# Attention probabilities and the residual transposed by VectorE blocks and strided DMA instead of TensorE

## The chip, the cores and the metric

The kernel runs on one core of one Trainium2 chip. The metric is the device time of one execution in microseconds (us). TensorE (PE in the profile) does the matrix products, VectorE (DVE) and ScalarE (ACT) the elementwise work, and SyncE (SP) issues nearly all DMAs; GpSimd (POOL) has next to nothing to do here. Each engine works through its own list of instructions in the order in which they were written down when the kernel was built, and an instruction that waits holds up all that stand behind it in that list.

## What is computed

Two layers of a sequence model on a sequence of 512 tokens of width 1024, each with an RMS norm ahead and a residual addition behind: first a state space mixer, then a latent attention mixer with 16 heads, and one more RMS norm at the end. The change is in the second layer. Cut to what matters:

```python
def mla_mixer(u, positions, in_w, q_norm_w, kv_norm_w, uq_w, ukv_w, out_w):
    proj = u @ in_w
    c_q, c_kv, k_r, z = proj[..., :o1], proj[..., o1:o2], proj[..., o2:o3], proj[..., o3:]
    q = (rms_norm(c_q, q_norm_w) @ uq_w).reshape(bsz, seq, 16, 192)
    kv = (rms_norm(c_kv, kv_norm_w) @ ukv_w).reshape(bsz, seq, 16, 256)
    ...
    o = causal_block_attention(q_full, k_full, v, 192 ** -0.5)   # p = softmax(q k^T); o = p v
    o = o.reshape(bsz, seq, 2048) * jax.nn.silu(z)
    return o @ out_w

h = h + mla_mixer(rms_norm(h, w), ...)
return rms_norm(h, final_norm_w)
```

## The kernel before, in words

All data are float32. A matrix product is made of three passes over parts `hi` and `lo` of its operands: ACT casts `hi`, DVE subtracts it from the source to get `lo`. This holds for weights (`split_weight`, tiles `raw`, `whi`, `wlo`) and for activations.

The first layer and the input projections work with features on the 128 partitions and the 512 tokens along the free dimension. The residual `h` (eight tiles of 128 features x 512 tokens) must be turned to tokens on partitions before the output projection, because `out_tok` makes its output that way. Before the change this is done in `mla`, in the loop over the six tiles of the first projection: behind each of the last four, eight transposes on PE through the identity matrix (line 682) go into two PSUM banks `pt`, ACT copies them to `ht` (L685), and SP writes `ht` to the DRAM buffer `hd` (L686). `out_tok` reads it back as `hr` (L924).

Attention works head by head. `score(h, b)` computes the scores of query block b (128 queries, b = 0 to 3) against keys 0 to 128(b+1), takes the softmax on DVE and ACT, and leaves the normalised probabilities `p` with queries on partitions. `product(h, kb)` needs them with keys on partitions. `turn(h, kb)` does this for key block kb: 4 - kb transposes on PE (L818, so 10 for a head) into a PSUM bank `pt`, then ACT casts `ph` (L822) and DVE subtracts to get `pl` (L823). Three matmuls of `product` (L836) then use `ph`, `pl` and the values `va`, `vb`.

The order of PE's instructions is written out by hand: PE's list is the order of the program text. The main loop runs over heads h = 0 to 15. An iteration feeds large matmuls (`front_a` or `front_b`, the projections for the next pair of heads, and `zgemm`, the gate; from head 11 on also the output projection), and `sched` puts pieces between them at fixed shares of the iteration: the scores of head h+1 at the shares `SC`, the turns of head h at `TU`, the products of head h at `PR`. `SF` holds the places of the scores of head 0. An iteration with even h has `front_a`, which also contains a rotation of half the query (`rope`): a PSUM result is copied to `rraw` (L732), four DMAs swap its quarters into `rsw` (L697), and DVE combines the two. An iteration with odd h has `front_b`.

The lists of DVE, ACT and SP are put in order by a scheduler at build time. On SP stand the weight loads (L263: `raw` has two buffers, and is free again once `wlo` is made), the DMAs of `rope` and those of `hd`.

Of the kernel before, what the change touches and what calls it, by code (L numbers as in the profile page):

```python
# [10 lines left out]
F32 = mybir.dt.float32  # L11
F32R = mybir.dt.float32r
AF = mybir.ActivationFunctionType
ALU = mybir.AluOpType

P = 128
T = 512
D = 1024
KD = D // P
NCH = T // P  # L20
# [3 lines left out]
MH = 16  # L24
QL, KVL = 384, 256
# [14 lines left out]
P1 = (1.0, 2.4, 3.8, 12.0, 18.2)  # L40
GN = 16.84
G7 = 33.0
SF = (0.02, 0.1, 2.1, 3.1)
SC = (0.0, 0.16, 0.25, 0.44)
TU = (0.02, 0.08, 0.38, 0.55)
PR = (0.3, 0.48, 0.65, 0.94)
KO = (3, 4, 5, 8, 10)
MID = 4
NU = 1
# [102 lines left out]
class Net:  # L152
# [497 lines left out]
    def mla(self):  # L650
        tc, nc, t, wk = self.tc, self.nc, self.t, self.wk
        v = nc.vector
# [3 lines left out]
        nc.sync.dma_start(con[:], t["con"][:, K_MASK:])  # L656
        self.mask, self.cosT, self.sinT = con[:, 0:T], con[:, T:2 * T], con[:, 2 * T:3 * T]
        hd = self.dram.tile([NCH, P, D], F32, name="hd")
        vh, vl = [], []
        for k in range(KD):  # L660
            h = self.h[k]
            a = self.act.tile([P, T], F32R, tag="ah", name=self.nm("vh"))
            b = self.act.tile([P, T], F32R, tag="al", name=self.nm("vl"))
# [6 lines left out]
        for i in range(6):  # L670
            w = self.weight("w", U_M1 + i)
            ps = self.bank("mm")
            self.run(self.gemm(ps[:], w, vh, vl, KD))
            if i == NU:
                pss = self.sumsq([h[:] for h in self.h], D, "b")
                r1 = self.rstd_of(pss, D)
            if i >= 2:
                c = i - 2
                for n in range(2):
                    pt = self.bank("pt")  # L680
                    for k in range(4):
                        nc.tensor.transpose(pt[:, k * P:(k + 1) * P], self.h[4 * n + k][:, c * P:(c + 1) * P],
                                            self.ident)
                    ht = wk.tile([P, T], F32, tag=("ph", "pl")[n], name=self.nm("ht"))
                    nc.scalar.copy(ht[:], pt[:])  # L685
                    nc.sync.dma_start(hd[c, :, n * T:(n + 1) * T], ht[:])  # L686
            pend.append(ps)
            while pend and i >= NU:
                o = self.o16.tile([P, T], F32, tag="o", name=self.nm("cq"))
                v.tensor_tensor(o[:], pend.pop(0)[:], r1[:], op=ALU.mult)  # L690
                cq.append(o)
# [15 lines left out]
        def zgemm(i):  # L707
            w = self.weight("w", U_MZ + i)
            ps = self.bank("mm")
            yield from self.gemm(ps[:], w, vh, vl, KD)  # L710
            z = self.o16.tile([P, T], F32, tag="o", name=self.nm("z"))
            v.tensor_tensor(z[:], ps[:], r1[:], op=ALU.mult)
            zt.append(z)
            yield 8 * 0.216
# [36 lines left out]
        def front_b(j):  # L751
            f = F[j]
            w = self.weight("ub", j)
            ps = self.bank("mm")
            yield from self.gemm(ps[:], w, qh, ql, 3)
            f["q", 1] = self.split(ps[:], "q", wk)
            yield 0.2
            ps = self.bank("mm")
            yield from self.gemm(ps[:], w, kh, kl, 2, 384)
            f["k", 1] = ksplit(ps[:])  # L760
            yield 1.3
            wh, wl = self.weight("uc", j)
            f["v"] = []
            for half in range(2):
                ps = self.bank("mm")
                for c2 in range(2):
                    c = 2 * half + c2
                    s = slice(c * P, (c + 1) * P)
                    seq = []
                    for k in range(2):  # L770
                        wc = slice(k * 256, k * 256 + 256)
                        seq += [(kh[k][:, s], wh[:, wc]), (kh[k][:, s], wl[:, wc]), (kl[k][:, s], wh[:, wc])]
                    for i, (a, b) in enumerate(seq):
                        nc.tensor.matmul(ps[:, c2 * 256:(c2 + 1) * 256], a, b, start=i == 0, stop=i == 5)  # L774
                va = wk.tile([P, T], F32R, tag="va", name=self.nm("va"), bufs=3)
                vb = wk.tile([P, T], F32R, tag="vb", name=self.nm("vb"), bufs=3)
                nc.scalar.copy(va[:], ps[:])
                v.tensor_tensor(vb[:], ps[:], va[:].bitcast(F32), op=ALU.subtract)
                f["v"].append((va, vb))
                yield 1.3  # L780

        probs = [[] for _ in range(MH)]

        def score(h, b):
            f, i = F[h // 2], h % 2
            (qa, qb), kk = f["q", i], f["k", i]
            r = f["r", i]
            n = P * (b + 1)
            s = slice(b * P, (b + 1) * P)
            ps = self.bank("s")  # L790
            if b:
                seq = [(qa, kk[:, 0]), (qa, kk[:, 1]), (qb, kk[:, 0]), (r, k1), (r, k2)]
                for k, (x, y) in enumerate(seq):
                    nc.tensor.matmul(ps[:, :n], x[:, s], y[:, :n], start=k == 0, stop=k == 4)  # L794
            else:
                both = ps[:, :2 * P].rearrange("p (a t) -> p a t", a=2)
                nc.tensor.matmul(both, qa[:, s], kk[:, :, :P], start=True, stop=False)
                nc.tensor.matmul(ps[:, :P], qb[:, s], kk[:, 0, :P], start=False, stop=False)
                nc.tensor.matmul(both, r[:, s], k12[:, :, :P], start=False, stop=True)
            p = self.res.tile([P, n], F32, tag="res", name=self.nm("p"))  # L800
            st = wk.tile([P, 4], F32, tag="st", name=self.nm("st"), bufs=8)
            mask = self.mask[:, T - n:]
            if b == 0:
                v.tensor_tensor(p[:], ps[:, P:2 * P], mask, op=ALU.add)
                mask = p[:]
            v.tensor_tensor_reduce(p[:], ps[:, :n], mask, -SCALE, 3.0e38, ALU.add, ALU.min, st[:, 0:1])  # L806
            self.E(p[:], p[:], AF.Exp, scale=-1.0, bias=st[:, 0:1], accum_out=st[:, 1:2])
            v.reciprocal(st[:, 2:3], st[:, 1:2])
            v.tensor_scalar(p[:], p[:], st[:, 2:3], None, op0=ALU.mult)
            probs[h].append(p)  # L810

        parts, acc = [[] for _ in range(MH)], {}

        def turn(h, kb):
            n = T - kb * P
            pt = self.bank("pt")
            for b in range(kb, NCH):
                nc.tensor.transpose(pt[:, (b - kb) * P:(b - kb + 1) * P], probs[h][b][:, kb * P:(kb + 1) * P],  # L818
                                    self.ident)
            ph = wk.tile([P, T], F32R, tag="ph", name=self.nm("ph"))  # L820
            pl = wk.tile([P, T], F32R, tag="pl", name=self.nm("pl"))
            nc.scalar.copy(ph[:, :n], pt[:, :n])  # L822
            v.tensor_tensor(pl[:, :n], pt[:, :n], ph[:, :n].bitcast(F32), op=ALU.subtract)  # L823
            parts[h].append((ph, pl))

        def product(h, kb):
# [13 lines left out]
        def chain(*gs):  # L840
            for g in gs:
                yield from g
# [4 lines left out]
            yield from self.out_tok(zt, 0, hd)  # L847

        def norm(tiles, n, cw):
            at = (wk, ("qh", "ql", "s2") if n == KVL else ("ph", "pl", "s2"))  # L850
            pss = self.sumsq([x[:] for x in tiles], n, "b", *at)
            r = self.rstd_of(pss, n, *at)
            hs, ls = [], []
            for i, x in enumerate(tiles):
                v.scalar_tensor_tensor(x[:], x[:], col(cw + i), r[:], op0=ALU.mult, op1=ALU.mult)
                a = wk.tile([P, T], F32R, tag="ch", name=self.nm("ch"), bufs=5)
                b = wk.tile([P, T], F32R, tag="cl", name=self.nm("cl"), bufs=5)
                nc.scalar.copy(a[:], x[:])
                v.tensor_tensor(b[:], x[:], a[:].bitcast(F32), op=ALU.subtract)
                hs.append(a)  # L860
                ls.append(b)
            return hs, ls
# [3 lines left out]
        qh, ql = norm(cq[:3], QL, C_QW)  # L866
# [14 lines left out]
        self.run(zgemm(3))  # L881
        zsilu(0)
        self.run(fa)
        self.run(front_b(0))
        self.sched(zgemm(4), [(x, functools.partial(score, 0, b)) for b, x in enumerate(SF)])
        for h in range(MH):
            if h and h % 4 == 0:
                zsilu(h // 4)
            feed, cost = [], 0.0
            j = h // 2 + 1  # L890
# [6 lines left out]
            if h >= 11:  # L897
                k = KO[h - 11]
                feed.append(itertools.islice(outg, k))
                cost += 1.3 * k  # L900
            at = SC if h + 1 < MH else ()
            pieces = [(x * cost, functools.partial(score, h + 1, b)) for b, x in enumerate(at)]
# [169 lines left out]
```

## Time and profile before

| | before |
|---|---|
| median of 3 runs | 840.51 us (840.49 to 840.99) |
| the profiled execution's own time | 840.15 us |
| its span in the profile | 838.3 us |
| PE, DVE, ACT busy, share of the span | 98%, 76%, 54% |
| DMA queue of SP (q1), share of 16 engines' span | 32.9% |
| granted TensorE clock | 0.998 |

The span is the time from the first to the last instruction in the profile; the execution's own time is 1.85 us longer. A busy share says how long an engine worked, not that the end depends on it. The chain of waits follows the end back from event to event and says which engine the time hangs on. A row of a list by line gives the line, the engine, the operation, the tile that is written and those that are read, shapes and count, then busy time and mean duration of one; a row of the timeline gives start, length and what ran; SPq is the issuing of DMAs on SP. The attention loop stands between about 500 and 784 us.

### The profile page before, as it was taken

The page shows a single profiled execution, that of the slowest core. Times are in us where ns is not written, and L with a number is a line of the kernel's source. Part 1 is how long each engine was busy: PE and PEld are TensorE (multiplying, and loading weights), DVE is VectorE, ACT ScalarE, POOL GpSimd, SP SyncE. Part 2 cuts the span into 40 slices and gives each one's busy share as a digit, 9 for nine tenths or more (in the row PEclk, how much of TensorE's full clock was granted, in tenths as well). Part 3 has the DMA queues.
Part 4 walks back from the last instruction along what each step waited for, and adds up shares of the span by engine and source line. Part 5 has one row for each costly group of instructions (what it writes and reads, how often), then busy time and mean ns, then how long its engine had stood idle before and what let it go on. Part 6 is the DMA issues. An engine that isn't in the chain of part 4 may idle for free.

```text
span 838.3 us, 11586 instructions
## 1 busy us (share of the span) xinstructions
PE 822.8 (98%) x4260; PEld 694.8 (83%) x4260; DVE 640.2 (76%) x1226; ACT 453.5 (54%) x802; POOL 0.2 (0%) x4
## 2 busy tenths in 40 slices
PE   7999999999999999999999999999999999999996
PEld 5887888888888888888888888888888888888885
DVE  7899898979788979776564887786767869675544
ACT  7567755545565657333354664456547557554233
POOL 0000000000000000000000000000000000000000
PEclk9999999999999999999999999999999999999999
DMA  6354543434242424323225242222221224331212
GB/s 227 102 186 145 153 150 106 147 101 128 98 151 76 151 87 137 121 95 101 90 86 176 79 129 64 77 65 73 73 64 56 89 75 157 100 100 53 92 59 100
DMA packets 35112, 90.55 MB, mean 108 GB/s; under 512 B 4784, under 2 KB 6320, under 8 KB 35056
## 3 DMA queue, kind: packets, MB, share of 16 engines
q1 hardware_dynamic: 34336, 88.77, 32.9%
q10 hardware_dynamic: 720, 1.05, 0.3%
q8 instruction: 33, 0.54, 0.3%
q14 instruction: 23, 0.19, 0.1%
HBM read 83.12 MB, written 4.33 MB: 104 GB/s over the span
## 4 chain that ended last, share of the span: by engine, by line
PE 91%; DVE 5%; DMA 2%; ACT 1%; issue 1%; SPq 0%; DVEq 0%; ACTq 0%
PE mm L291 54%; PE ot L942 11%; PE s L794 5%; PE mm L300 4%; PE po L836 4%; PE mm L774 3%; PE pt L818 2%; PE yd L138 2%; PE yd L291 1%; PE aux L130 1%; PE aux L105 1%; DMA x<-in_x_dram 1%; PE aux L77 1%; PE aux L89 1%; DMA L<-ac_d 1%; DVE wlo L273 1%
## 5 line engine op out<-in xcount | busy, mean ns | idle before, releaser
L272 ACT CAST whi<-raw 128x1024 fp32r<-128x1024 f32 (+3 forms) x132 | 127.0, 965 | 214.7 <-PE mm L291 177.4
L273 DVE TENSOR_TENSOR wlo<-raw,whi 128x1024 fp32r<-128x1024 f32 (+3 forms) x132 | 146.8, 1115 | 56.1 <-ACT whi L272 55.8
L291 PE MATMUL mm<-ah,whi 128*128 128x512 f32 x384 | 153.9, 401 | 0.0
L291 PE MATMUL mm<-ah,wlo 128*128 128x512 f32 x384 | 150.1, 391 | 0.4 <-DVE wlo L273 0.4
L291 PE MATMUL mm<-al,whi 128*128 128x512 f32 x384 | 149.8, 390 | 0.0
L291 PE MATMUL mm<-vh,whi 128*128 128x512 f32 x224 | 89.6, 400 | 0.9 <-ACT whi L272 0.9
L291 PE MATMUL mm<-vh,wlo 128*128 128x512 f32 x224 | 87.8, 392 | 0.7 <-DVE wlo L273 0.7
L291 PE MATMUL mm<-vl,whi 128*128 128x512 f32 x224 | 87.5, 391 | 0.0
L291 PEld LDWEIGHTS mm<-ah,wlo 128*128 128x128 f32 x384 | 72.1, 188 | 16.0 <-DVE wlo L273 0.8
L291 PEld LDWEIGHTS mm<-ah,whi 128*128 128x128 f32 x384 | 72.2, 188 | 15.5 <-issue 1.4
L291 PEld LDWEIGHTS mm<-al,whi 128*128 128x128 f32 x384 | 72.2, 188 | 14.4 <-DVE al L312 0.3
L942 PE MATMUL ot<-whi,ah 128*128 128x512 f32 (+1 forms) x136 | 52.3, 384 | 0.0
L942 PE MATMUL ot<-whi,al 128*128 128x512 f32 (+1 forms) x136 | 51.4, 378 | 0.0
L942 PE MATMUL ot<-wlo,ah 128*128 128x512 f32 (+1 forms) x136 | 51.4, 378 | 0.0
L291 PEld LDWEIGHTS mm<-vh,wlo 128*128 128x128 f32 x224 | 42.0, 188 | 10.8 <-DVE wlo L273 1.5
L291 PEld LDWEIGHTS mm<-vh,whi 128*128 128x128 f32 x224 | 42.1, 188 | 9.2 <-ACT whi L272 1.1
L223 ACT ACTIVATE p<-p,st 128x128 f32<-128x128 f32 (+1 forms) x64 | 36.1, 564 | 25.1 <-DVE st L806 25.0
L291 PEld LDWEIGHTS mm<-vl,whi 128*128 128x128 f32 x224 | 42.2, 188 | 7.2
L822 ACT CAST ph<-pt 128x512 fp32r<-128x512 f32 (+1 forms) x64 | 26.5, 422 | 33.2 <-PE pt L818 32.8
L291 PE MATMUL mm<-ch,whi 128*128 128x512 f32 x104 | 42.6, 409 | 0.0
L291 PE MATMUL mm<-ch,wlo 128*128 128x512 f32 x104 | 40.8, 392 | 0.0
L291 PE MATMUL mm<-cl,whi 128*128 128x512 f32 x104 | 40.7, 392 | 0.0
(225 smaller groups left out, 1642.6 us busy)
## 6 DMA issues: line engine op xcount, KB each, us to landing
raw<-in_w_dram SPq DMA_DIRECT2D x100, 512.0 KB, 3.3
L<-ac_d SPq DMA_DIRECT2D x32, 256.0 KB, 3.8
E<-ea_d SPq DMA_DIRECT2D x32, 128.0 KB, 3.3
raw<-in_ua_dram SPq DMA_DIRECT2D x8, 512.0 KB, 3.3
raw<-in_ub_dram SPq DMA_DIRECT2D x8, 320.0 KB, 2.9
x<-in_x_dram SPq DMA_DIRECT2D x8, 256.0 KB, 4.3
res<-in_x_dram SPq DMA_DIRECT2D x8, 256.0 KB, 3.3
hd<-ht SPq DMA_DIRECT2D x8, 256.0 KB, 2.3
```

The costliest lines, as they stand in the source:

```text
L138: nc.tensor.matmul(yd[64 * h:64 * h + 64, s], self.xdt[j][:, c, h, :], self.L[2 * j + h][:, s], start=True, stop=True)
L223: i = self.nc.scalar.activation(out, in_, func, **k)
L272: nc.scalar.copy(hi[:, a:b], raw[:, a:b])
L273: nc.vector.tensor_tensor(lo[:, a:b], raw[:, a:b], hi[:, a:b].bitcast(F32), op=ALU.subtract)
L291: self.nc.tensor.matmul(ps, a, b, start=i == 0, stop=i == len(seq) - 1)
L300: self.nc.tensor.matmul(p, seq[i][0], seq[i][1], start=i == 0, stop=i == 3 * ks - 1)
L774: nc.tensor.matmul(ps[:, c2 * 256:(c2 + 1) * 256], a, b, start=i == 0, stop=i == 5)
L794: nc.tensor.matmul(ps[:, :n], x[:, s], y[:, :n], start=k == 0, stop=k == 4)
L818: nc.tensor.transpose(pt[:, (b - kb) * P:(b - kb + 1) * P], probs[h][b][:, kb * P:(kb + 1) * P], self.ident)
L822: nc.scalar.copy(ph[:, :n], pt[:, :n])
L836: nc.tensor.matmul(po[:, kb * P:], x, y, start=kb == 0 and k == 0, stop=kb == NCH - 1 and k == 2)
L942: nc.tensor.matmul(ps[:, a:b], x, y, start=start and i == 0, stop=stop and i == 5)
```

## The change

The transposes on PE go. A block of probabilities `p` is turned in blocks of 32 x 32 by one DVE instruction into a new tile `pb` (two buffers); this leaves each 32 x 32 block turned in its place, and four DMAs for each `pb`, one for each 32 partitions, write the blocks to their places in a DRAM buffer `pd` (one for even, one for odd heads) as pieces of 32 floats, 128 bytes each. `turn` reads a key block of `pd` into `pl` with one DMA; ACT casts `ph` from it, and DVE makes `pl` in place. `pl` now has one buffer for each kb. The residual goes the same way: eight DVE transposes of 128 x 512 and 32 DMAs of 128-byte pieces into `hd`, spread over the same loop. The tables move: the scores of the next head stand earlier in an iteration, the products later. The scores of head 0 move from `zgemm(4)` into `front_b(0)`. The temporary tiles of the query's norm use other tags.

```diff
-SF = (0.02, 0.1, 2.1, 3.1)
-SC = (0.0, 0.16, 0.25, 0.44)
-TU = (0.02, 0.08, 0.38, 0.55)
-PR = (0.3, 0.48, 0.65, 0.94)
+SF = (0.6, 1.0, 2.0, 3.2)
+SC = (0.0, 0.1, 0.18, 0.28)
+TU = (0.04, 0.14, 0.4, 0.6)
+PR = (0.52, 0.66, 0.8, 0.96)
...
+        turned = hd[:].rearrange("c (j a) d -> a (c j) d", a=32)
...
             if i >= 2:
-                c = i - 2
-                for n in range(2):
-                    pt = self.bank("pt")
-                    for k in range(4):
-                        nc.tensor.transpose(pt[:, k * P:(k + 1) * P], self.h[4 * n + k][:, c * P:(c + 1) * P],
-                                            self.ident)
-                    ht = wk.tile([P, T], F32, tag=("ph", "pl")[n], name=self.nm("ht"))
-                    nc.scalar.copy(ht[:], pt[:])
-                    nc.sync.dma_start(hd[c, :, n * T:(n + 1) * T], ht[:])
+                for k in (2 * i - 4, 2 * i - 3):
+                    ht = wk.tile([P, T], F32, tag="ph", name=self.nm("ht"))
+                    v.transpose(ht[:], self.h[k][:])
+                    for b in range(4):
+                        m = slice(32 * b, 32 * b + 32)
+                        nc.sync.dma_start(turned[:, :, k * P + 32 * b:k * P + 32 * b + 32],
+                                          ht[m, :].rearrange("a (j b) -> a j b", b=32))
...
-        probs = [[] for _ in range(MH)]
+        pd = [self.dram.tile([T, T], F32, name=f"pd{i}") for i in range(2)]
...
-            probs[h].append(p)
+            pb = wk.tile([P, T], F32, tag="pb", name=self.nm("pb"))
+            v.transpose(pb[:, :n], p[:])
+            turned = pd[h % 2][:].rearrange("(j a) q -> a j q", a=32)
+            for i in range(4):
+                q = b * P + 32 * i
+                nc.sync.dma_start(turned[:, :n // 32, q:q + 32],
+                                  pb[32 * i:32 * i + 32, :n].rearrange("a (j q) -> a j q", q=32))
...
         def turn(h, kb):
             n = T - kb * P
-            pt = self.bank("pt")
-            for b in range(kb, NCH):
-                nc.tensor.transpose(pt[:, (b - kb) * P:(b - kb + 1) * P], probs[h][b][:, kb * P:(kb + 1) * P],
-                                    self.ident)
+            pl = wk.tile([P, n], F32R, tag=f"pl{kb}", name=self.nm("pl"), bufs=1)
+            nc.sync.dma_start(pl[:].bitcast(F32), pd[h % 2][kb * P:(kb + 1) * P, kb * P:])
             ph = wk.tile([P, T], F32R, tag="ph", name=self.nm("ph"))
-            pl = wk.tile([P, T], F32R, tag="pl", name=self.nm("pl"))
-            nc.scalar.copy(ph[:, :n], pt[:, :n])
-            v.tensor_tensor(pl[:, :n], pt[:, :n], ph[:, :n].bitcast(F32), op=ALU.subtract)
+            nc.scalar.copy(ph[:, :n], pl[:].bitcast(F32))
+            v.tensor_tensor(pl[:], pl[:].bitcast(F32), ph[:, :n].bitcast(F32), op=ALU.subtract)
...
-            at = (wk, ("qh", "ql", "s2") if n == KVL else ("ph", "pl", "s2"))
+            at = (wk, ("qh", "ql", "s2"))
...
-        self.run(front_b(0))
-        self.sched(zgemm(4), [(x, functools.partial(score, 0, b)) for b, x in enumerate(SF)])
+        self.sched(chain(front_b(0), zgemm(4)), [(x, functools.partial(score, 0, b)) for b, x in enumerate(SF)])
```

SP's list in the iteration of head 6, an even one, had only weight loads and the four DMAs of `rope` before:

```order
L263 DMA raw_5729<-in_ub_dram 128x640
L263 DMA raw_5848<-in_uc_dram 128x512
L263 DMA raw_5909<-in_w_dram 128x1024
L697 DMA rsw_5775<-rraw_5773 32x512 x4
L263 DMA raw_5991<-in_ua_dram 128x1024
```

In the same iteration SP now has the following list, in which `pd_4157` is the buffer of head 7, written in four sets of four, and `pd_4156` that of head 6, read as `pl`:

```order
L263 DMA raw_5823<-in_ub_dram 128x640
L814 DMA pd_4157<-pb_5847 32x4x32 x4
L822 DMA pl_5853<-pd_4156 128x512
L814 DMA pd_4157<-pb_5870 32x8x32 x4
L696 DMA rsw_5881<-rraw_5879 32x512 x4
L822 DMA pl_5895<-pd_4156 128x384
L814 DMA pd_4157<-pb_5919 32x12x32 x4
L814 DMA pd_4157<-pb_5944 32x16x32 x4
L822 DMA pl_5960<-pd_4156 128x256
L263 DMA raw_5965<-in_uc_dram 128x512
L822 DMA pl_5988<-pd_4156 128x128
L263 DMA raw_6017<-in_w_dram 128x1024
```

The reads of head 6 stand between the writes of head 7: the third read is behind 16 writes and the four DMAs of `rope`. This is so in the iterations of heads 0, 2, 4, 6, 8 and 10, and without `rope` in that of head 13; in that of head 11 the last read alone is behind the writes. In the other odd iterations all four reads of a head stand ahead of the 16 writes of the next one.

On PE, where the scores of the first query block stand in the same iteration, seven transposes for key blocks 0 and 1 followed before:

```order
L797 MATMUL s_5742<-k_5590,qh_5579 128x256
L798 MATMUL s_5742<-k_5590,ql_5580 128x128
L799 MATMUL s_5742<-k_4353,s_1075_5410 128x256
L818 MATMUL pt_5753<-ident,p_5552 128x128
L818 MATMUL pt_5753<-ident,p_5599 128x128
L818 MATMUL pt_5753<-ident,p_5611 128x128
L818 MATMUL pt_5753<-ident,p_5674 128x128
L818 MATMUL pt_5762<-ident,p_5599 128x128
L818 MATMUL pt_5762<-ident,p_5611 128x128
L818 MATMUL pt_5762<-ident,p_5674 128x128
```

The scores of the second block follow at once now:

```order
L796 MATMUL s_5836<-k_5682,qh_5671 128x256
L797 MATMUL s_5836<-k_5682,ql_5672 128x128
L798 MATMUL s_5836<-k_4339,s_1072_5488 128x256
L793 MATMUL s_5858<-k_5682,qh_5671 128x256 x2
L793 MATMUL s_5858<-k_5682,ql_5672 128x256
L793 MATMUL s_5858<-k_4339,s_1072_5488 128x256 x2
```

Nothing else is taken out of PE's list in an iteration. At its end, the products of key blocks 2 and 3 (`pl_5960` and `pl_5988` are what SP reads above) now stand next to each other:

```order
L291 MATMUL mm_5971<-vh_3866,wlo_5826 128x512
L838 MATMUL po_5978<-ph_5962,va_5762 128x256
L838 MATMUL po_5978<-ph_5962,vb_5763 128x256
L838 MATMUL po_5978<-pl_5960,va_5762 128x256
L838 MATMUL po_5978<-ph_5990,va_5762 128x128
L838 MATMUL po_5978<-ph_5990,vb_5763 128x128
L838 MATMUL po_5978<-pl_5988,va_5762 128x128
```

In this even iteration the products of blocks 2 and 3 are the last of PE's work, behind all of `zgemm`.

## The prediction

> **What bounds the kernel now.** I read the page's busy times first, then its chain of waits by engine, then PE's waits.
>
> ```profile
> PE 822.8 (98%) x4260; PEld 694.8 (83%) x4260; DVE 640.2 (76%) x1226; ACT 453.5 (54%) x802; POOL 0.2 (0%) x4
> PE 91%; DVE 5%; DMA 2%; ACT 1%; issue 1%; SPq 0%; DVEq 0%; ACTq 0%
> PE mm L300 <- ACT whi L272: 4.8, 1, 4.8
> PE mm L291 <- DVE wlo L273: 1.0, 3, 0.5
> ```
>
> PE is busy for 98% of the span, 91% of the chain lies on it, and its two longest waits (total, times, longest) come to 5.8 us, one of them with 4.8 us at the start. In the attention loop it does not wait at all. So what is taken out of PE's list shortens the time, as long as nothing new makes PE wait; and every new wait costs in full.
>
> **What the change removes.** The transposes' price is read from the chain, where each piece is the time that PE's list moves on, not from the mean duration, since matmuls overlap.
>
> ```profile
> 443.03 0.87 PE pt L682 x8
> 507.71 0.12 PE s L797
> 508.06 0.76 PE pt L818 x7
> 515.14 0.22 PE pt L818 x2
> 519.80 0.11 PE pt L818
> 524.72 0.12 PE s L797
> ```
>
> Eight transposes of the residual take 0.87 us, and the ten of a head 0.76 + 0.22 + 0.11 = 1.09 us: 0.109 us each. There are 32 + 160 = 192 of them, so PE loses 192 x 0.109 = **20.9 us** of work. The two rows of L797 mark the same place in two iterations: an even one lasts 17.0 us, and without its transposes 15.9 us. If all that is new were hidden, 840.15 - 20.9 = 819 us would remain.
>
> **What it adds on DVE and ACT.** A transpose in DVE does not occur in the trace. The nearest rows read and write the same shapes in SBUF, one input:
>
> ```profile
> L809 DVE TENSOR_SCALAR p<-p,st 128x512 f32<-128x512 f32 x16 | 7.7, 481 | 0.2
> L809 DVE TENSOR_SCALAR p<-p,st 128x128 f32<-128x128 f32 x16 | 4.4, 278 | 0.0
> L823 DVE TENSOR_TENSOR pl<-pt,ph 128x512 fp32r<-128x512 f32 x16 | 11.0, 690 | 3.7 <-ACT ph L822 3.7
> L312 DVE TENSOR_TENSOR al<-z,ah 128x512 fp32r<-128x512 f32 x16 | 10.8, 686 | 9.4 <-ACT ah L311 9.4
> 549.00:567.00 18.00, 18.00 (x103) 15.74 (x103) 15.53 (x36) 9.80 (x21) 0.00 (x0) 1.00 0.23 73
> 567.00:584.00 17.00, 17.00 (x93) 14.71 (x92) 10.10 (x29) 12.34 (x24) 0.00 (x0) 1.00 0.23 67
> ```
>
> From 0.28 us (128 columns) to 0.48 us (512), a head's four take about 1.5 us; with the two-input row, 0.69 us for 512, they would take some 2 us. The last two rows are two iterations (length, then busy PE, PEld, DVE, ACT): DVE works 25.6 of 35 us. With 3 to 4 us more it works 29 of the 33 us that remain: covered, though with little to spare. Subtracting from SBUF instead of PSUM costs the same (686 and 690 ns), so `pl` stays as it is, and so does `ph`. ACT's eight copies of the residual fall away; ACT was not what PE waited for there.
>
> **What it adds on SP.** A head now issues 16 writes and 4 reads more. What an issue takes when others stand right ahead of it:
>
> ```profile
> 58.70 1.75 SPq L627 DMA_DIRECT2D L<-ac_d  x4
> 61.12 0.59 SPq L124 DMA_DIRECT2D E<-ea_d  x1
> 61.76 0.59 SPq L123 DMA_DIRECT2D E<-ea_d  x1
> 580.44 2.41 SPq L697 DMA_DIRECT2D rsw<-rraw  x4
> hd<-ht SPq DMA_DIRECT2D x8, 256.0 KB, 2.3
> raw<-in_uc_dram SPq DMA_DIRECT2D x8, 256.0 KB, 2.7
> ```
>
> A DMA over 128 partitions takes 1.75 / 4 = 0.44 us. One over 64 (`E`: 61.12 to 61.76) or 32 partitions (`rsw`: 2.41 us for four, with the gaps between) takes 0.63 us. No row has a DMA over 32 partitions in many pieces. I bound a write by 0.44 us below and by 0.9 us above (an estimate: half as much again as the row of the same 32 partitions), and take **0.63 us**, since that row has its partitions. A head's writes then hold SP for 10 us, and with reads, loads and `rope` some 13.5 of 16 us.
>
> Does this delay PE? In an odd iteration the reads are ahead of the writes, so they are in time. In an even one SP's order is: 4 writes, read 0, 4 writes, 4 DMAs of `rope`, read 1, 8 writes, read 2. The first write needs the softmax of the first query block of head h+1, whose scores PE makes in this same iteration; product 2 of head h, at the end of the same iteration, needs read 2. Nothing done earlier can loosen that. Its length, from the iteration's first matmul:
>
> ```profile
> 518.41 1.39 PE mm L291 x6
> 519.91 0.36 PE po L836 x3
> 581.47 0.51 PE L794 MATMUL s<-k,s 128*128 128x384 f32 x2
> 583.55 0.42 DVE L809 TENSOR_SCALAR p<-p,st 128x384 f32<-128x384 f32 x1
> L822 ACT CAST ph<-pt 128x256 fp32r<-128x256 f32 x16 | 5.9, 370 | 0.4
> L823 DVE TENSOR_TENSOR pl<-pt,ph 128x256 fp32r<-128x256 f32 x16 | 6.7, 417 | 0.0
> ```
>
> - six matmuls (1.39) and the first block's scores (0.35, as 0.12 + 0.06 + 0.17 in the chain): 1.7 us
> - softmax: 2.0 us, as from the end of the scores at 581.98 to the end of the scaling at 583.97 for 384 columns
> - the transpose of 128 columns: 0.3 us, so the first write is issued at 4.0 us
> - 20 DMAs over 32 partitions at 0.63 and reads 0 and 1 at 0.44: 13.5 us
> - read 2 to landing, as the load of the same size class: 2.7 us
> - `ph` and `pl` of 256 columns: 0.8 us; six matmuls of products 2 and 3: 0.6 us
>
> The sum is 21.6 us, against 15.9 us of PE's own work: PE waits **5.7 us** in each of six iterations (heads 0 to 10), 34 us. The iteration of head 13 has no `rope` (four DMAs, 2.5 us, less), and that of head 11 has only its last read behind the writes; by the same sum I put them at about 3 us each. Together 40 us of new waits.
>
> While read 2 is late, ACT stands at the cast of `ph`, and behind it on ACT are the casts of the next weights. These are not late: a weight is loaded two ahead, and SP gets to the loads right after read 2, an iteration before PE needs them. The residual's 32 writes hold SP for 20 us, spread over the about 80 us in which the `h` tiles are finished and the first projection runs; I cost them at nothing, under weights loaded ahead. If that cover is gone, the price is a few waits of 2.5 us, one set of four writes each.
>
> **The DMA engines.** The data come in 128-byte pieces: 40 x 128 for a head, since ten blocks of 128 x 128 have four pieces a row, so 82,000 for the heads and 16,000 for the residual.
>
> ```profile
> q1 hardware_dynamic: 34336, 88.77, 32.9%
> q10 hardware_dynamic: 144, 0.00, 0.8%
> ```
>
> The first row is the whole span: 0.329 x 16 x 838.3 / 34336 = 128 ns for a packet of 2.6 KB on average. The second is ACT's queue in the first 10 us, 144 packets of a few bytes: 0.008 x 16 x 10 / 144 = 8.9 ns. A head's 5,120 pieces, 320 on each of 16 engines, would take 2.9 us at the lower and 41 us at the upper price. Pieces of 128 bytes are nearest the lower: no bound. It would become one from about 40 ns, where 320 x 0.04 = 13 us and the 4 us of loads (0.23 x 17) fill an iteration. The Trainium skill speaks against the change here: "DMA: Bandwidth & Descriptors", Specifications, asks for pieces of 512 bytes or more for full rate, since smaller ones are read, modified and written. By it, and at the rate of the first row, a piece would cost an estimated 25 ns (128 x 512 / 2600) and a head's 8 us: more, but still beside the chain on SP, so the sum would stay. No row shows a small write to DRAM, so the trace can neither confirm nor deny it.
>
> **The rivals.**
> 1. *SP is quick enough.* If a write issues like a 128-partition DMA (0.44 to 0.45 us), each even iteration's chain is 20 x 0.18 = 3.6 us shorter, and those of 11 and 13 by 2.9 us. That leaves 40 - 21.6 - 5.8 = 13 us, plus some 2 us because the second write set then waits for its own transpose: 840.15 - 20.9 + 15 = **834 us**, faster. The mechanism is the same chain; it decides at about 0.50 us a write (six times 20 and two times 16 are 152 issues, and the 859 - 840 = 19 us between slower and same are 0.13 us each, under 0.63). For it: 128-partition DMAs do issue so. Against: 32 and 64 partitions alike take 0.63.
> 2. *All is hidden,* **819 us**, if writes also overlap `rope` or land far sooner. Against it: 23 issues in line at 0.33 us, the shortest single issue, are already 7.6 us of the chain.
> 3. *Writes cost more than any row shows,* by their 128 to 512 pieces each. At 0.9 us: 20 x 0.27 = 5.4 us more in six iterations and 4.3 in two: 859 + 41 = **900 us**. Against it: `L`, with 128 pieces, issues quicker than `rsw` with 32.
>
> **How the numbers follow.** The forecast is 840.15 - 20.9 + 40 = **859 us**; it is made against the profiled execution's 840.15 us (span 838.3), 0.36 us under the median of 840.51, which is nothing beside the unknowns. Its own range, 1.5 us more or less on each of eight waits, is 847 to 871. Chances: the forecast 0.52, rival 1 0.23, rival 2 0.08, rival 3 0.17. The range reaches from a little under rival 1 to rival 3: 831 to 900. About 0.2% is what a measurement of this kernel can tell from no change. Faster takes rival 2, most of rival 1 and a little of the forecast's tail: 0.30; same 0.04; slower 0.66.
>
> **What would show it.** After the change PE's waits should name ACT or DVE's `ph` and `pl` ahead of `po`, 5 to 6 us in each even iteration, and SP should issue writes back to back there, at 0.6 us or more each. The iterations with odd heads up to 9 should last about their transposes' share (1.1 us) less than before. If a write issues in under 0.5 us, or reads land in well under 2.3 us, the sign is wrong; if PE waits in odd iterations as well, the price of a write is higher than I took.

## The result and the profile after

The changed kernel takes 884.71 us (median of 4 runs, 879.96 to 888.15) beside 840.57 us for the kernel before (840.49 to 840.99): 1.052 times as long, with a 95% interval of 1.0466 to 1.0574. It is 44 us slower; the forecast was 19 us slower. Its four runs differ by 8 us, and the longer ones have the lower granted clock (0.989 at 879.96 us, 0.975 at 888.15). The profiled execution took 882.81 us, with a span of 881.0 us and a granted clock of 0.984.

The page's busy times and the shares of its chain of waits:

```profile
PE 822.9 (93%) x4068; PEld 680.0 (77%) x4068; DVE 673.0 (76%) x1298; ACT 450.6 (51%) x794; POOL 0.2 (0%) x4
PE 75%; DVE 8%; DMA 7%; SPq 4%; ACT 3%; issue 2%; DVEq 0%; ACTq 0%
```

The two longest waits of PE (total, times, longest):

```profile
PE po L838 <- ACT ph L824: 31.2, 25, 9.2
PE po L838 <- DVE pl L825: 8.9, 16, 1.4
```

PE lost its 192 transposes and is yet busy for as long as before (822.9 beside 822.8 us). Its idle time grew from 838.3 - 822.8 = 15.5 to 881.0 - 822.9 = 58.1 us, and 40.1 us of that stand in two rows that were not there before: products waiting for `ph` and `pl`. By the timeline they stand ahead of all four products of a head: 9.5 us in all ahead of the first, 8.6 ahead of the second, 9.5 ahead of the third and 12.6 ahead of the fourth (9.2 of these in one iteration, that of head 11). The chain now leaves PE for a quarter of the span.

The length of an iteration is the distance between the first score matmuls of successive heads in the timeline. The following table has PE's own work (the length before, less 1.09 us of transposes) beside the length after; an iteration bears the number of the head whose products it makes.

| iterations | before | own work | after | longer than own work by | forecast |
|---|---|---|---|---|---|
| 0, 2, 4, 6, 8, 10 (mean) | 17.0 | 15.9 | 22.56 | 6.7 each | 5.7 each |
| 1, 3, 5, 7, 9 (mean) | 17.8 | 16.7 | 16.73 | 0 | 0 |
| 11 | 16.5 | 15.4 | 27.2 | 11.8 | 3 |
| 12 | 17.0 | 15.9 | 17.4 | 1.5 | 0 |
| 13 | 19.2 | 18.1 | 25.3 | 7.2 | 3 |

In iteration 12 PE waits for nothing; its 1.5 us come from the clock, as shown below.

Iteration 2, at 20.8 us the shortest of the six even ones, shows the chain of the prediction. From the timeline (start, length, what ran, and in brackets the idle time ahead and what ended it): SP's list, then ACT, then PE.

```profile
549.68 1.73 SPq L814 DMA_DIRECT2D pd<-pb  x4
551.57 0.34 SPq L822 DMA_DIRECT2D pl<-pd  x1
552.13 1.78 SPq L814 DMA_DIRECT2D pd<-pb  x4
554.01 2.41 SPq L696 DMA_DIRECT2D rsw<-rraw  x4
556.52 0.53 SPq L822 DMA_DIRECT2D pl<-pd  x1
557.14 4.08 SPq L814 DMA_DIRECT2D pd<-pb  x8
561.32 0.45 SPq L822 DMA_DIRECT2D pl<-pd  x1
561.82 0.43 SPq L263 DMA_DIRECT2D raw<-in_uc_dram  x1
562.35 0.38 SPq L822 DMA_DIRECT2D pl<-pd  x1
...
563.72 0.41 ACT L824 CAST ph<-pl 128x256 fp32r<-128x256 f32 x1 [1.41 <-PE mm L291]
564.66 0.62 ACT L272 CAST whi<-raw 128x512 fp32r<-128x512 f32 x1 [0.53 <-DMA raw<-in_uc_dram]
565.18 0.29 ACT L824 CAST ph<-pl 128x128 fp32r<-128x128 f32 x1
...
566.26 0.33 PE L838 MATMUL po<-pl,va 128*128 128x128 f32 x1 [0.29 <-DVE pl L825]
```

SP issues almost without a pause from 549.68 to the third read at 561.32: the four reads of the head are spread between the 16 writes of the next one and the four DMAs of `rope`. A write takes 1.73 / 4 = 0.43 to 4.08 / 8 = 0.51 us. The last product's matmul comes at 566.26, 20.6 us after the iteration's first matmul at 545.66. In longer iterations the second set of writes waits for its transpose as well: SP stands still for 2.8 us ahead of it in iteration 0, and in iteration 4 the set takes 3.42 us where it takes 1.78 here.

### The profile page after: what moved, and what is told of

It is laid out like the page before. It is cut to its first block, busy times and chain, and to the rows that moved or that the text cites. A ratio compares the mean times of both kernels' runs of the same rounds, so it can differ in the third digit from the quotient of the medians.

```text
span 881.0 us, 11831 instructions
## 1 busy us (share of the span) xinstructions
PE 822.9 (93%) x4068; PEld 680.0 (77%) x4068; DVE 673.0 (76%) x1298; ACT 450.6 (51%) x794; POOL 0.2 (0%) x4
## 3 DMA queue, kind: packets, MB, share of 16 engines
q1 hardware_dynamic: 145312, 109.76, 43.4%
## 4 chain that ended last, share of the span: by engine, by line
PE 75%; DVE 8%; DMA 7%; SPq 4%; ACT 3%; issue 2%; DVEq 0%; ACTq 0%
PE mm L291 47%; PE ot L943 8%; PE s L793 4%; PE mm L300 4%; SPq L814 2%; PE po L838 2%; PE mm L773 2%; PE yd L138 2%; DMA raw<-in_w_dram 2%; DMA raw<-in_uc_dram 1%; PE yd L291 1%; PE aux L130 1%; PE aux L105 1%; DMA x<-in_x_dram 1%; ACT whi L272 1%
## 5 line engine op out<-in xcount | busy, mean ns | idle before, releaser
L291 PEld LDWEIGHTS mm<-ah,whi 128*128 128x128 f32 x384 | 72.2, 188 | 15.4 <-issue 1.4
L838 PE MATMUL po<-ph,va 128*128 128x512 f32 (+1 forms) x64 | 22.5, 352 | 31.2 <-ACT ph L824 31.2
L824 ACT CAST ph<-pl 128x512 fp32r<-128x512 f32 (+1 forms) x64 | 28.4, 456 | 43.9 <-DMA pl<-pd 31.5
L838 PEld LDWEIGHTS po<-ph,va 128*128 128x128 f32 x64 | 12.2, 191 | 42.4 <-ACT ph L824 40.9
```

The costliest lines, as they stand in the source:

```text
L291: self.nc.tensor.matmul(ps, a, b, start=i == 0, stop=i == len(seq) - 1)
L824: nc.scalar.copy(ph[:, :n], pl[:].bitcast(F32))
L838: nc.tensor.matmul(po[:, kb * P:], x, y, start=kb == 0 and k == 0, stop=kb == NCH - 1 and k == 2)
```

## The experiments

**The change in its two halves, and its tables.** In e3 the kernel before gets the residual's new way alone; in e2 the change keeps the residual on TensorE; in e8 the kernel before gets the new tables (and the scores of head 0 in `front_b(0)`) alone.

For e3, against the kernel before:

```diff
-                    pt = self.bank("pt")
-                    for k in range(4):
-                        nc.tensor.transpose(pt[:, k * P:(k + 1) * P], self.h[4 * n + k][:, c * P:(c + 1) * P],
-                                            self.ident)
...
+                    v.transpose(ht[:], self.h[k][:])
+                    for b in range(4):
+                        m = slice(32 * b, 32 * b + 32)
+                        nc.sync.dma_start(turned[:, :, k * P + 32 * b:k * P + 32 * b + 32],
+                                          ht[m, :].rearrange("a (j b) -> a j b", b=32))
```

> The kernel before with only the residual turned by DVE and written by 32 DMAs of 128-byte pieces; the probabilities are turned on TensorE as before. Theory (the writes are covered, and PE loses 32 transposes, 3.5 us): 837 us. In the trace of the change the stage's mark came only 0.8 us earlier, so the gain may be as small as 0.8: 836.5 to 840. Rival (the writes on SP delay weights): over 841 us, with PE waiting for a cast of weights in the first projection.

e2 is the reverse of this edit in the changed kernel (one of its two `ht` takes the buffers of `pb`, since those of `pl` are no longer there).

> The change with the residual turned on TensorE as before; only the probabilities go through DVE and DRAM. Theory (all of the loss is in the attention loop, and the residual's 32 writes are hidden or give back a part of what their transposes cost): 882 to 888 us, as the change or up to 4 us slower. Rival (the residual's writes hold up loads of weights and so carry part of the loss): under 878 us.

For e8, against the kernel before:

```diff
-SF = (0.02, 0.1, 2.1, 3.1)
-SC = (0.0, 0.16, 0.25, 0.44)
-TU = (0.02, 0.08, 0.38, 0.55)
-PR = (0.3, 0.48, 0.65, 0.94)
+SF = (0.6, 1.0, 2.0, 3.2)
+SC = (0.0, 0.1, 0.18, 0.28)
+TU = (0.04, 0.14, 0.4, 0.6)
+PR = (0.52, 0.66, 0.8, 0.96)
```

> The kernel before with the four new tables and the scores of head 0 moved into the projection of the second query, but with all transposes on TensorE as before. Theory (the tables cost nothing by themselves; they only say where a late read is felt): 838 to 842 us. Rival (the scores of the next head, ahead of the casts in DVE's and ACT's lists, make products late by themselves): over 845 us, with PE waiting for the probabilities' hi and lo parts ahead of its products.

e3 took 836.62 us, 0.9952 times the kernel before (0.9937 to 0.9967): 4.0 us faster, so the residual's half pays what its transposes cost, and its 32 writes are hidden. e2 took 893.0 us (2 runs), further above the change than expected. 3.5 us are the transposes; the granted clock, 0.976 beside 0.984, makes up to 0.008 x 893 = 7 us more. All of the loss is thus with the probabilities, none with the residual. It is not all in the loop: in e2 the first scores of head 1, with which iteration 0 begins, stand at 512.8 us, where the kernel before has them at 507.6. e8 took 842.19 us, 1.0022 times (1.0012 to 1.0032), 0.2 us above what was expected: the tables and the new place of head 0's scores cost 1.6 us together.

**Another order on SP.** In e1 all reads of a head are written down ahead of the next head's writes, and `turn` keeps only the cast and the subtraction. In e7 the reads go to GpSimd's queue.

For e1:

```diff
+        def read(h):
+            for kb in range(NCH):
+                n = T - kb * P
+                pl = wk.tile([P, n], F32R, tag=f"pl{kb}", name=self.nm("pl"), bufs=1)
+                nc.sync.dma_start(pl[:].bitcast(F32), pd[h % 2][kb * P:(kb + 1) * P, kb * P:])
+                got[h, kb] = pl
...
             at = SC if h + 1 < MH else ()
+            read(h)
```

For e7:

```diff
-            nc.sync.dma_start(pl[:].bitcast(F32), pd[h % 2][kb * P:(kb + 1) * P, kb * P:])
+            nc.gpsimd.dma_start(pl[:].bitcast(F32), pd[h % 2][kb * P:(kb + 1) * P, kb * P:])
```

> The change with one thing moved: the four reads of a head's probabilities are written down at the start of its iteration, ahead of all writes of the next head, in place of one ahead of each cast; casts, writes and products stay where they are. Theory (order on SP: in even iterations the reads of head h stand behind the writes of head h+1 that this iteration has yet to make): the waits of PE ahead of its products go from 64 us to under 8, and the time falls by 50 to 62 us, to 823 to 835 us, under the kernel before. Rival (the price of the 128-byte pieces themselves: they are slow to issue and to land, or slow the other loads, wherever they stand): the waits move to other instructions, PE still loses over 30 us, and the time stays over 855. Rival (SP's issue time as a sum, 30 DMAs a head): SP is as busy as before the move, the reads of the next head wait for its writes, and the time is 850 or more.

> The change with the reads alone issued by GpSimd, each free to go as soon as its own head's writes have landed; writes, rotation and loads stay on SP. Theory: as e1, since the reads leave the place behind the writes: even iterations lose their waits, and the odd ones then wait for the rotation, behind writes on SP, 4 to 5 us in PE: 870 to 910 us. If the odd iterations don't wait, the rotation's delay in e1 came from the reads ahead of it (1.8 us) and not from the writes, and the time is under 850.

e1 took 909.23 us, 1.0823 times (1.0804 to 1.0842), slower than the change by 25 us: the theory, as written there, fell. Its even iterations did lose their waits (16.3 to 17.9 us), but the odd ones now last 25 to 26 us. The waits of PE in e1:

```profile
PE s L798 <- DVE s L737: 19.0, 7, 4.2
PE mm L773 <- ACT whi L272: 15.6, 7, 2.2
```

A piece of SP's list in its iteration 0, behind eight writes:

```profile
515.01 2.41 SPq L696 DMA_DIRECT2D rsw<-rraw  x4
517.68 4.06 SPq L814 DMA_DIRECT2D pd<-pb  x8
521.79 0.49 SPq L263 DMA_DIRECT2D raw<-in_uc_dram  x1
```

PE no longer waits for `ph` and `pl`, but for `s1` and `s2`, which need the rotation, and for `whi` of the weight `uc`: the DMAs of both stand behind writes. e7 took 894.81 us (2 runs), in the expected range, with the same two waits (16.4 and 17.5 us).

In e4 the rotation's four DMAs go to GpSimd; e5 has both edits, e1's and e4's.

```diff
-                nc.sync.dma_start(sw[32 * i:32 * i + 32, :], raw[32 * j:32 * j + 32, :])
+                nc.gpsimd.dma_start(sw[32 * i:32 * i + 32, :], raw[32 * j:32 * j + 32, :])
```

> The change with the four DMAs that swap the quarters for the rotation issued by GpSimd, which is idle, in place of SP. Theory (SP's list is the chain): SP's list is 2.4 us shorter ahead of read 1 in six even iterations and that of head 11 is unchanged in kind, so PE waits 6 x 2.4 = 14 us less: 865 to 875 us. Rival (the chain is not SP's issuing but the landing of writes and the order of ACT's casts): within 4 us of the change, 880 to 889.

> The reads written down first, as in e1, and the four DMAs of the rotation issued by GpSimd, as in e4. In e1 the even iterations lost their waits (16.3 to 17.9 us), and the odd ones waited instead for the rotation's result, whose DMAs stood on SP behind eight writes. In e4 the rotation left SP, and the reads still waited, for a last set of writes that waited for its DVE transpose. Theory (two users of SP's list, each late by itself as soon as the other is cured): with both cured, even and odd iterations up to 10 last 16 to 18 us, and only those of heads 11 and 13 wait: 825 to 845 us. Rival (DVE is the bound, with transposes, rotation and softmax in one list): the scores or products still wait for DVE, 5 us or more in every second iteration, and the time is over 870.

Both theories fell. e4 took 897.63 us (2 runs), outside what either side expected. DVE's and SP's rows of the timeline in iteration 2 of e4:

```profile
561.22 0.70 DVE L810 STREAM_TRANSPOSE pb<-p 128x512 f32<-128x512 f32 x1
...
557.08 6.81 SPq L814 DMA_DIRECT2D pd<-pb  x8
563.98 0.44 SPq L822 DMA_DIRECT2D pl<-pd  x1
```

With the rotation's DMAs elsewhere, its instructions stand earlier in DVE's list, and the last transpose of the next head comes at 561.22, where the change had it at 557.28. SP stands in the middle of its eight writes until then (6.81 us instead of 4.08), and the third read stands behind them. e5 took 899.72 us, 1.0696 times (1.0661 to 1.0731), in the rival's range, though DVE is only a part of the reason. The rotation is cured there; PE waits for the weight `uc` (L773) and for `pl`:

```profile
PE mm L773 <- ACT whi L272: 17.6, 7, 4.2
PE po L845 <- DVE pl L832: 9.2, 8, 2.6
```

SP's list in iteration 0 of e5:

```profile
516.03 11.19 SPq L814 DMA_DIRECT2D pd<-pb  x9
527.32 0.44 SPq L263 DMA_DIRECT2D raw<-in_uc_dram  x1
```

The nine writes hold SP for 11.19 us, where 9 x 0.5 = 4.5 would do if their data were ready, and the load of `uc` waits with them. So it is less the sum of issue times than the place: whatever stands behind a write waits until that write's softmax and transpose are done. Reads, rotation and weights each stand there in turn.

**The writes on another queue.** e6 leaves the order as it is and takes the writes alone off SP's list.

```diff
-                nc.sync.dma_start(turned[:, :n // 32, q:q + 32],
+                nc.gpsimd.dma_start(turned[:, :n // 32, q:q + 32],
                                   pb[32 * i:32 * i + 32, :n].rearrange("a (j q) -> a j q", q=32))
```

> The change with all 16 writes of each head issued by GpSimd in place of SP; reads, rotation and weight loads stay on SP. Theory (what delays PE is what stands behind the writes on SP): reads, rotation and loads no longer queue behind writes, and the time is 820 to 845 us, unless GpSimd issues a write slower than SP's 0.5 us. Rival (the writes' own price, on the way from DVE to DRAM): as the change, 875 or more.

e6 took 851.88 us (2 runs), 33 us less than the change, and 7 us more than expected. The writes are as many as before, and GpSimd issues them no faster. From its timeline:

```profile
560.93 2.57 POOL L814 DMA_DIRECT2D pd<-pb  x4 [4.25 <-DVE pb L810]
```

PE's waits in e6:

```profile
PE po L838 <- ACT ph L824: 9.7, 13, 1.9
PE po L838 <- DVE pl L825: 9.0, 15, 1.5
```

A write takes 2.57 / 4 = 0.64 us there, but stands in nobody's way: PE waits 18.7 us ahead of its products, not 40.1. One thing changes besides the place. The DMA queues of the change (packets, MB, share), then those of e6:

```profile
q1 hardware_dynamic: 145312, 109.76, 43.4%
q1 hardware_dynamic: 59296, 99.26, 38.1%
q0 software_dynamic: 8192, 10.50, 4.9%
```

The 10.5 MB of the writes are 86,016 packets on SP's queue (q1) and 8,192 on GpSimd's (q0). The writes don't land sooner for it: in 1.9 to 3.0 us in the median of each size in e6, in 1.5 to 1.9 in the change. A write in e6 is thus issued more slowly and lands later, and the time is still 33 us shorter. This is the run that shows the cause: not what a write costs by itself, but what is queued behind it. What the fewer packets do for the reads (those of 256 KB land in 3.0 us in the median, not 4.2; those of 128 KB in 3.7, not 3.5) was not separated. What remains stands mostly ahead of a head's first product, and e10 moves the products later.

```diff
-PR = (0.52, 0.66, 0.8, 0.96)
+PR = (0.66, 0.76, 0.86, 0.96)
```

> The writes issued by GpSimd, as in e6, and the products later in an iteration, at the shares 0.66, 0.76, 0.86 and 0.96. In e6 nearly all that was left of PE's waits stood ahead of a head's first product, 0.3 to 1.8 us twice an iteration. Theory (the first read is late by less than 2 us, and a later product hides it): 825 to 838 us, under the kernel before. Rival (a later product only moves the wait, since the reads follow SP's order and buffers): 845 to 855 us.

e10 took 836.79 us, 0.9958 times the kernel before (0.9943 to 0.9973): faster by 3.8 us. This is no more than e3 gains with the residual alone. The 17.4 us of the probabilities' transposes are still given back, now in many small waits among the products: an even iteration lasts 17.3 us on average, where PE's own work is 15.9. Of the 16 that the list of waits shows ahead of products, 15 are for `pl`, which DVE makes. In iteration 2 the last `ph` is ready at 554.1, but its `pl` stands in DVE's list behind the scaling and the transpose of the next head, and DVE has no pause there:

```profile
553.79 0.30 ACT L824 CAST ph<-pl 128x128 fp32r<-128x128 f32 x1 [0.43 <-PE po L838]
555.40 0.70 DVE L810 STREAM_TRANSPOSE pb<-p 128x512 f32<-128x512 f32 x1
556.03 0.25 DVE L825 TENSOR_TENSOR pl<-pl,ph 128x128 fp32r<-128x128 f32 x1
556.33 0.33 PE L838 MATMUL po<-pl,va 128*128 128x128 f32 x1 [0.24 <-DVE pl L825]
```

So with the writes out of the way, most of the waits that are left name DVE, and here it is its list that makes them. No run takes anything off it in the loop.

**The tables again.** e11 is the change with the four tables and the line for the scores of head 0 turned back (the lines with a minus in the change's diff). e12 is e10 with `SF` and that line turned back, and the products later still:

```diff
-PR = (0.66, 0.76, 0.86, 0.96)
+PR = (0.7, 0.79, 0.88, 0.97)
```

> The change with the four tables of the kernel before and the scores of head 0 where they were; the probabilities and the residual still go through DVE and DRAM. In even iterations SP's order is now 4 writes, reads 0 and 1, the rotation's 4, 8 writes, read 2, 4 writes, read 3. Theory (a product of head h waits for a read behind writes of head h+1): the last scores stand 0.16 of an iteration later and products 0 to 2 earlier, so the waits are as long or longer than in the change: 880 to 905 us. Rival (the new tables, with scores of the next head sooner, are what brought the writes ahead of the reads, and the old ones loosen it): under 870 us.

> As e10, with the scores of head 0 where the kernel before has them, and the products at 0.70, 0.79, 0.88 and 0.97. In e8 the new place of the scores of head 0 cost about 1.5 us, and in e10 PE still waits some 8 us ahead of products. Theory: 1.5 us less from the front and 1 to 3 from the products: 832 to 835.5 us, the fastest of all. Rival (what is left hangs on DVE's list, and later products move it to the next iteration): 836 to 840 us.

e11 took 902.28 us (2 runs), within the expected range: with the old tables PE waits 45.3 us for `ph` alone (31.2 in the change). The new tables help this way of transposing; they don't suffice. e12 took 842.3 us, 1.0025 times (1.001 to 1.004), above what either side expected, so its theory fell: the front gains, and the iteration of head 0, which now has less time for the writes of its own head, loses more (22.2 us instead of 17.7).

**The clock.** In the change PE's granted clock falls in places. Two windows of iteration 4 (length, then busy PE, PEld, DVE, ACT, POOL, the granted clock, DMA share, GB/s):

```profile
583.00:599.00 16.00, 12.93 (x62) 10.06 (x61) 11.20 (x30) 6.26 (x15) 0.00 (x0) 1.00 0.41 91
599.00:602.50 3.50, 3.50 (x9) 2.64 (x10) 2.38 (x4) 1.24 (x2) 0.00 (x0) 0.56 0.61 107
```

Matmuls on both sides of a wait, from the timeline:

```profile
595.24 0.40 PE L291 MATMUL mm<-vh,whi 128*128 128x512 f32 x1
595.47 0.39 PE L291 MATMUL mm<-vl,whi 128*128 128x512 f32 x1
598.87 0.44 PE L838 MATMUL po<-ph,va 128*128 128x384 f32 x1 [2.11 <-ACT ph L824]
599.95 0.63 PE L291 MATMUL mm<-vh,whi 128*128 128x512 f32 x1
600.38 0.63 PE L291 MATMUL mm<-vl,whi 128*128 128x512 f32 x1
```

Ahead of the wait of 2.11 us matmuls follow each other at 0.23 us, behind it at 0.43. e9 puts idle matmuls where PE waits.

```diff
+            fill = {0: 2, 1: 2, 2: 10, 3: 4}[kb] if h % 2 == 0 and h < 12 else 6 if h == 13 else 30 * (h == 11 and kb == 3)
+            if fill:
+                pw = self.bank("pw")
+                for k in range(fill):
+                    nc.tensor.matmul(pw[:], qh[0][:, :P], qh[1][:], start=k == 0, stop=k == fill - 1)
             ph, pl = parts[h][kb]
```

> The change with matmuls whose result nothing reads put on TensorE ahead of the products where it waits (18 in each even iteration up to 10, 30 ahead of the last product of head 11, 24 in that of 13, 0.227 us each, less than the wait at that place). Theory (the waits of PE halve its granted clock for the next 3.4 us or more, and that is a cost beside the waits themselves): the granted clock stays at 1.0 through the attention loop, and the time falls by 2 to 8 us against the change, though PE has 162 matmuls more: 874 to 883 us. Rival (the clock falls for another reason, such as the load on the DMA engines): the clock falls as in the change, to 0.98 or less, and the time is 882 to 905 us.

e9 took 878.55 us (2 runs, 876.7 and 880.39) with a granted clock of 0.996: 6.2 us less than the change by the medians, though PE has 162 matmuls more. The last 100 us of the attention loop in the change, then in e9:

```profile
700.00:800.00 100.00, 79.11 (x373) 64.95 (x373) 67.92 (x161) 46.66 (x97) 0.00 (x0) 0.91 0.56 149
700.00:800.00 100.00, 94.37 (x459) 78.25 (x458) 69.20 (x165) 47.28 (x99) 0.00 (x0) 0.98 0.57 152
```

The DMA share is the same in both, so DMA load is not what lowers the clock; PE's idling is. But the length of a single wait does not decide it: in iteration 0 of the change, a wait of 2.15 us ends at 522.14, and the clock stays at 1.00 behind it:

```profile
522.50:526.00 3.50, 3.41 (x15) 2.35 (x13) 2.20 (x5) 1.24 (x2) 0.00 (x0) 1.00 0.75 122
```

Iteration 12 shows the clock's price by itself, since PE waits for nothing there. In the change it begins at half clock, behind the wait of iteration 11 (0.90 on average), and lasts 17.4 us; in e9 it lasts 15.8, PE's own work:

```profile
753.04:770.40 17.36, 17.36 (x79) 14.87 (x78) 12.26 (x32) 7.15 (x17) 0.00 (x0) 0.90 0.35 69
752.70:768.50 15.80, 15.80 (x79) 13.51 (x78) 12.80 (x34) 6.93 (x17) 0.00 (x0) 1.00 0.40 81
```

So the clock is a cost of its own, but how much of the 44 us it makes is not settled. The change's four runs (from 879.96) and e9's two overlap, and the two profiled executions differ by 2.4 us only: iterations 11 and 12 are 3.3 and 1.6 us shorter in e9, the six even ones up to 10 are 2.6 us longer together.

## Why the prediction was half right

- **The bound and the sign.** PE's list was the bound, and new waits cost in full. The wait named (PE's products on `ph` and `pl`), its place (even iterations) and its cause (reads behind the next head's writes in SP's list) are in the trace, and e6 shows the cause: with the writes on another queue 33 of 44 us are gone. Odd iterations up to 9 are 1.1 us shorter, as forecast.
- **What the change removes.** 20.9 us of transposes went; e3 gains in full for the residual's share. But the sum took PE's remaining work at a full clock. In the change it runs partly at half clock after its waits, which e9 puts at 2.4 us by the profiled executions, or 6.2 by the medians. The Trainium skill has this rule in "TensorE: Matmul & The Clock Gate", "Why this matters for your kernels": no idle gaps over about 3 us between bursts of matmuls, or the clock halves. The trace agrees that the clock halves with PE's idling, but not on the length: it fell after a wait of 2.11 us in iteration 4, and in iteration 6 after waits of 0.93, 0.20 and 0.29 us in a row.
- **SP's issue time.** 0.63 us a write was too high: it is 0.43 to 0.51. So rival 1 had its condition (about 0.50 us a write) and still did not come about, and the test "if a write issues in under 0.5 us, the sign is wrong" was itself wrong. Two errors met here: 16 cheaper writes shorten an even iteration's chain by 16 x 0.16 = 2.6 us, and in iteration 2 the chain did reach its third `ph` at 563.72 - 545.66 = 18.1 us, against 20.2 forecast. But the sum ended too early, behind read 2: read 3 stands behind the load of `uc`, the cast of `uc` stands ahead of the last `ph` on ACT and on DVE, and the last matmul starts 2.5 us after the third `ph`, where 1.4 us were to cover all. Products 0 and 1 waited too, for reads behind one and two sets of writes, where the sum has only product 2 wait. With all this and the half clock in it, the mean came out at 6.7 us against 5.7 (iteration 2: 4.9); that it came so near is in part luck. (SP's "some 13.5 of 16 us" is a slip: 20 DMAs at 0.63 and seven at 0.44 make 15.7 in an even iteration. Nothing else rests on it.)
- **Heads 11 and 13: the largest miss.** The step "by the same sum I put them at about 3 us each" failed; they last 11.8 and 7.2 us longer than PE's own work. In iteration 11, whose first matmul is at 724.40, SP's list, ACT and PE run as follows:

```profile
735.16 5.28 SPq L814 DMA_DIRECT2D pd<-pb  x8
740.48 1.00 SPq L925 DMA_DIRECT2D hr<-hd  x2
741.58 0.38 SPq L263 DMA_DIRECT2D raw<-in_w_dram  x1
742.05 0.38 SPq L822 DMA_DIRECT2D pl<-pd  x1
...
747.55 1.04 ACT L272 CAST whi<-raw 128x1024 fp32r<-128x1024 f32 x1 [8.59 <-DMA raw<-in_w_dram]
748.50 0.29 ACT L824 CAST ph<-pl 128x128 fp32r<-128x128 f32 x1
...
748.84 0.48 PE L838 MATMUL po<-ph,va 128*128 128x128 f32 x1 [9.22 <-ACT ph L824]
```

  The read of the last key block goes out at 742.05, behind all 16 writes, two reads of `hr` and the load of a weight, and by the trace it lands 5.7 us later, at 747.8; the last `ph` needs it, and PE waits 9.22 us for that. The mechanism is the one forecast, the terms were too small: the writes end 740.44 - 724.40 = 16.0 us after the start, not 4.0 + 16 x 0.63 = 14.1; what else stands ahead of the read takes 1.6 us; the landing takes 3.0 us more than the 2.7 reckoned; and behind the wait PE runs at half clock. "These are not late", of weights, failed too: the load, out at 741.58, lands at about 747.5, and ACT does its cast ahead of `ph`. But that costs only the 0.7 us from 747.8 to 748.5. In iteration 13 the longest wait, 2.60 us, is for the third `ph`, whose read goes out behind 16 writes 17.5 us after the iteration's first matmul, where the sum's terms give 15.0.
- **The sum, put right.** 6 x 6.7 + 11.8 + 1.5 + 7.2 = 60.7 us take the place of 40 (the half clock is in them); heads 11 and 13 alone are 13 of these 20.7 us. The part ahead of head 0's iteration gains 0.7 us instead of the 3.5 of its transposes; 1.3 of the 2.8 us are there in e8 too, by the new place of head 0's scores, and the rest was not separated. That is 20.7 + 2.8 = 23.5 of the 23.7 us between the forecast's 19 and the 42.7 us that the spans differ by.
- **The DMA engines.** They were no bound, as forecast. SP's queue has 145,312 - 34,336 = 110,976 packets more than before, and they take (0.434 x 881.0 - 0.329 x 838.3) x 16 = 1,705 us more of the 16 engines' time, or 15 ns each (an estimate from the pages of the two profiles); the forecast put the limit at about 40.

What stays open: how much of the 60.7 us is due to reads that land later than the 2.7 us taken (3.5 to 4.3 us in the median). In iteration 11 it was 3.0 us for the one read that counts; elsewhere it was not separated from the order on SP.

## What to carry to other kernels

A DMA that waits for late data holds up all that stands behind it in its queue's list, so before new DMAs go on a queue, list who else lives there, and follow the last one as well as the first: moving one of them forward only shows the next. A transfer that waits belongs on a queue where nothing behind it is urgent. Moving work off the bounding engine pays only if that engine stays fed; its idle gaps cost twice where its clock falls with them. And when the queue is cured, the next list is worth a look: here it was, for most of the waits left, that of DVE, to which the work had been moved.

## What the runs showed of the hardware

- In the change PE's granted clock fell to half in four places of the attention loop, for about 3.4 us in three of them (0.56 over 599.00 to 602.50), in or behind waits of 2.11, 2.60 and 9.22 us and behind three of 0.93 us and less; a wait of 2.15 us left it at 1.00. With PE kept busier it fell once (e9).
- A DMA of 32 partitions in 128-byte pieces issues on SP in 0.43 to 0.51 us, quicker than one of 32 whole rows (2.41 / 4 = 0.60 us for `rsw`), and on GpSimd in 0.55 to 0.64 us (2.18 / 4 to 2.57 / 4 in e6).
- The profile counts 86,016 packets for the probabilities' 10.5 MB of writes on SP's queue and 8,192 on GpSimd's; those from GpSimd landed later (1.9 to 3.0 us) than those from SP (1.5 to 1.9).
- DVE's transposes of 32 x 32 blocks take 0.31 us (128 columns) to 0.71 us (512), up to half as much again as the scaling of the same shape:

```profile
L810 DVE STREAM_TRANSPOSE pb<-p 128x512 f32<-128x512 f32 x16 | 11.3, 707 | 0.2
L810 DVE STREAM_TRANSPOSE pb<-p 128x128 f32<-128x128 f32 x16 | 4.9, 309 | 0.3
```
